# Shift states of a hybrid encoder step written out through TensorE, and half A's first layer norm transposed in the dense PSUM banks

## The chip, the cores and the metric

The kernel is one launch on one core of a Trainium2 chip. The metric is device time in microseconds (us) of that launch. A run's time is that of one execution; the profile is of one more execution. About 0.5% (some 15.5 us here) is the least difference that a measurement of this kernel can tell from none.

## The reference, cut to what matters

A two-layer streaming encoder runs over 1024 new frames of one stream (the prompt, from empty states) and over the next 64 frames of another stream (the sample, from given states). Layer 0 is one input projection that feeds two mixers (RWKV-7 and gated linear attention, GLA), then an output projection; layer 1 is chunk-band attention. Each layer ends with a SwiGLU feed-forward, and each of the four sub-blocks with a layer norm of the residual sum. Everything is float32.

```python
def rwkv7_time_mix(pa, shift0, wkv0, mu, ...):
    prev = jnp.concatenate([shift0[:, None, :], pa[:, :-1]], axis=1)
    xs = pa + (prev - pa) * mu
    ...
    return y, wkv.astype(wkv0.dtype), pa[:, -1]      # pa[:, -1]: the shift state, 1792 numbers

# run_trunk, per layer
x = layer_norm(DEEPNORM_ALPHA * x + mix, P['ln1_w'][layer], P['ln1_b'][layer])
x = layer_norm(DEEPNORM_ALPHA * x + swiglu(x, ...), P['ln2_w'][layer], P['ln2_b'][layer])
```

Two of the twelve outputs are shift states: the last projected row of mixer A, 1792 numbers, once for the prompt and once for the sample.

## The kernel before

The 1088 tokens are split in two halves. Half A holds the first 384 prompt frames and the 64 sample frames (448 columns), half B the other 640 prompt frames. TensorE (PE) works in fp32 split in a high and a low part, so every dense product is three matmuls: high by high, high by low, low by high (lines 124 to 126 with weights stationary, 135, 136 and 138 with tokens stationary). The weights' split is one ACT cast (L101) and one subtraction on DVE (L106) or GpSimd (POOL, L108).

The order in the first part of the program: input projection of half A (`inproj_rwkv`, `inproj_gla`), the mixers of half A beside it, input projection of half B, and then, from about 540 us, three kinds of work woven together: the mixers of half B (the generators `r` for RWKV, 20 units of two 64-token chunks for four head pairs, and `g` for GLA, 20 units), the output projection of half A (`proj(0, ...)`, matrix `w_om`), its layer norm (`layer_norm(0, acc0, "ln1", 0)`), and from there the feed-forward of half A (`ffn(0, 0, ...)`). The program gives the work in that order of text; the framework's scheduler then lays out a fixed order for each engine by its own estimate of times. Each engine runs its list in order and waits on semaphores, so an instruction that waits holds everything behind it on its engine. Nearly all transfers are issued by SyncE (SP), in order too. Each transfer takes one of eight completion semaphores in turn, and the issue of a transfer waits until the earlier one with the same semaphore has landed.

**Shift states.** `shift_evac` copies the last column of each of the 14 projected tiles, one number per partition, into `shS` (sample, L284) and `shP` (prompt, L290), each 128 partitions by 14. Lines 1377 and 1378 write them to the outputs, which are 14 rows of 128: with partitions along the row, each transfer consists of 1792 pieces of 4 bytes.

**PSUM.** The eight banks are given by tags. `gp` has three banks in rotation (`bank()`, tile name `gps`): every dense product takes one, and it is free again when DVE or ACT has read it. `sp_ps` has five banks for the mixers (`sbank(name)`): one for tag a (`pa`, `pb`, `pt`), one for b (`pz`), two for c (`ps`, `py`), one for d (GLA's `gpa`, `gps`, `gpy`). The GLA products are also named `gps`; they are lines 738 to 740.

**The layer norm** of a token tile (line 875 on): statistics on DVE (L884, L886), 1/std on POOL (L888, L889), scaling in two halves (DVE L892, then ACT L894 and POOL L895 for the first half, DVE L897 for the second), then for each half four transposes on PE (L902) into a bank that `self.tpsum()` gives, and the split of the transposed half into high and low (ACT L113, DVE L114), which is the feed-forward's input. In this part `tpsum` is `sbank("tps")`, which falls to tag d, the one bank of GLA.

**The projection** runs over its matrix in two groups of 4 row blocks; per group and token tile it has two products of 512 columns (12 matmuls each), each added to the residual by DVE (L825 in the first group, L827 in the second, L829 for the sample tile's second part). After the second product of a token tile in the second group comes `after(i)`, the layer norm of that tile. Half A has four token tiles, so the norm has eight transposed halves.

```python
for i, t0, m in toks:
    for nh in range(2):
        part(ws[nh], nh, i, t0, m)     # bank(), 12 matmuls, DVE add
    after(i)                           # layer norm of the tile: two tpsum() banks
```

Of the kernel before, what the change touches and what calls it, by code (L numbers as in the profile page):

```python
# [10 lines left out]
F32 = mybir.dt.float32  # L11
# [10 lines left out]
NM = max(NA, NB)  # L22
# [61 lines left out]
class Kern:  # L84
# [134 lines left out]
    def mixer_consts(self, pool, tmp):  # L219
        nc, V = self.nc, self.V  # L220

        def ld(n, src, shape, dt=F32):
            t = pool.tile(shape, dt, name=n, tag=n)
            (nc.sync if n == "vec" else nc.sync).dma_start(t, src)
            setattr(self, n, t)
            return t

        vec = ld("vec", self.a["vec"], [128, NVEC])
        for n, (o, w) in VO.items():
            setattr(self, n, vec[:, o : o + w])  # L230

        def mk(n, src, s, b):
            t = pool.tile([128, src.shape[1]], F32, name=n, tag=n)
            V.tensor_scalar(t, src, s, b, op0=ALU.mult, op1=ALU.add)
            setattr(self, n, t)

        nc.sync.dma_start(self.ident, self.a["c_ident"])
        mk("omu", self.mu, -1.0, 1.0)
        mk("w0h", self.w0, 0.5, 0.0)
        mk("a0h", self.a0, 0.5, 0.0)  # L240
        mk("kah", self.ka, 0.5, 0.0)
        mk("kah1", self.ka, -0.5, 1.0)
        mk("gnwh", self.gnw, 0.5, 0.0)
        self.shA = pool.tile([128, 14], F32, name="shA", tag="shA")
        self.shS = pool.tile([128, 14], F32, name="shS", tag="shS")
        self.shP = pool.tile([128, 14], F32, name="shP", tag="shP")
        for n, sh in (("bdk", [128, 128]), ("mab", [128, 128]), ("mup", [128, 128]), ("mk2", [128, 128]), ("m65", [128, 130]),
                      ("m64", [128, 128]), ("s8", [128, 32]), ("eye16", [16, 256])):
            ld(n, self.a["c_" + n], sh)
        self.u8 = pool.tile([128, 192], U8, name="u8", tag="u8")  # L250
        raw = tmp.tile([128, NM], F32, tag="sq", name="u8raw", bufs=3)[:, :192]
        nc.sync.dma_start(raw, self.a["c_u8"])
        V.tensor_copy(self.u8, raw)
        z = tmp.tile([128, NM], F32, tag="sq", name="zero", bufs=3)[:, :256]
        self.G.memset(z, 0.0)
        for i in range(self.NSL):
            nc.sync.dma_start(self.mats(self.t_d[i], 2), z.rearrange("p (c f) -> p c f", c=2))
            nc.sync.dma_start(self.s_d[i].rearrange("(p f) -> p f", p=128), z[:, : 2 * SST // 128])
        for n in ("w2z", "a2z", "g2"):
            ld(n, self.a[n], [128, 512])  # L260
        self.bd = self.bdk
        self.bd3 = self.bd.rearrange("p (b s) -> p b s", b=2)
# [1077 lines left out]
    def run(self):  # L1340
        nc, tc, a = self.nc, self.tc, self.a
# [17 lines left out]
        one = es_one.enter_context(tc.tile_pool(name="one", bufs=1))  # L1359
# [14 lines left out]
        self.load_xt(1)  # L1374
        self.inproj_gla(1, one)
        self.inproj_rwkv(1, one)
        nc.sync.dma_start(a["s_shift"].rearrange("c p -> p c"), self.shS)
        nc.sync.dma_start(a["p_shift"].rearrange("c p -> p c"), self.shP)
        es_one.close()
        self.load_xt(0, self.yg_d, (4, 5, 6, 7, 0, 1, 2, 3), pool=yp)  # L1380
        es_yr.close()
# [14 lines left out]
        for _ in range(self.PRE):  # L1396
            next(r)
            next(g)
        self.proj(0, acc0, "w_om", self.layer_norm(0, acc0, "ln1", 0), pa)
        for _ in r:  # L1400
            next(g, None)
        for _ in g:
# [212 lines left out]
```

## Time and profile before

| what | value |
|---|---|
| runs, us | 3109.51, 3102.37, 3113.97 (median 3109.51) |
| profiled execution, us | 3102.95 |
| its span, first to last instruction, us | 3101.2 |
| mean granted TensorE clock, share of full speed | 0.977 |
| PE busy, us (share of span) | 3007.5 (97%) |
| DVE busy | 2016.0 (65%) |
| POOL, ACT busy | 1366.7 (44%), 1270.8 (41%) |

The profiled execution is 6.6 us (0.2%) below the median of the runs and 0.6 us above the fastest of them. A busy PE is not a PE at its peak: the granted clock has two levels, 2.4 GHz (1.0 in the rows) and 1.2 GHz (0.5), and a matmul at the lower one takes nearly twice as long. In the rows below PEld is TensorE's weight load and SPq a transfer's issue on SP's queue; `out<-in` are the program's tiles.

### The profile page before, as it was taken

What the parts mean: (1) busy time and instruction counts of PE and PEld (TensorE: products, weight loads), DVE (VectorE), ACT (ScalarE), POOL (GpSimd) and SP (SyncE); (2) the same over time, 40 slices, a digit from 0 to 9 for tenths busy, and PEclk for the clock granted to TensorE, in tenths of its full rate; (3) what the DMA queues carried; (4) which work ended last, traced back from release to release, by engine and by line L of the source; (5) the groups of instructions that cost most, each with busy time, mean ns of one, the idle gap of its engine ahead of it and who ended that gap; (6) DMA issues with size and microseconds to landing.
All of it is one profiled execution on the core that took longest, in us unless ns stands there. A gap on an engine that the chain in (4) does not pass through costs nothing.

```text
span 3101.2 us, 50069 instructions
## 1 busy us (share of the span) xinstructions
PE 3007.5 (97%) x17468; PEld 2676.5 (86%) x17468; DVE 2016.0 (65%) x4941; ACT 1270.8 (41%) x2761; POOL 1366.7 (44%) x1489
## 2 busy tenths in 40 slices
PE   8999999899999999999999999999999999899998
PEld 7888888688888888798999898898899988899987
DVE  5677875879898764455554466245566668866667
ACT  4454554344454334243443132355444434333322
POOL 2354534444454334343342233244445546654444
PEclk9999999889999999999999999999899999999999
DMA  6553334533533228343342222866454443322212
GB/s 195 148 161 115 109 110 124 146 104 106 151 105 106 91 97 294 118 153 120 113 134 98 82 95 101 247 200 175 121 153 135 117 175 122 122 86 80 98 68 75
DMA packets 298492, 399.29 MB, mean 129 GB/s; under 512 B 125504, under 2 KB 218552, under 8 KB 298240
## 3 DMA queue, kind: packets, MB, share of 16 engines
q1 hardware_dynamic: 297088, 393.48, 41.2%
q8 instruction: 138, 2.26, 0.3%
q10 hardware_dynamic: 1152, 2.62, 0.2%
q14 instruction: 114, 0.93, 0.1%
HBM read 323.63 MB, written 75.51 MB: 129 GB/s over the span
## 4 chain that ended last, share of the span: by engine, by line
PE 77%; DVE 8%; DMA 7%; POOL 2%; issue 2%; ACT 2%; SPq 1%; POOLq 0%; ACTq 0%; DVEq 0%
PE gps L124 11%; PE gps L126 11%; PE gps L125 11%; PE gps L135 7%; PE gps L136 7%; PE gps L138 7%; PE gps L1065 3%; PE gps L1066 3%; PE gps L1067 3%; PE op L1328 2%; PE tp L1302 2%; DVE t L549 1%; DVE x L551 1%; PE sps L1286 1%; PE sps L1287 1%
## 5 line engine op out<-in xcount | busy, mean ns | idle before, releaser
L108 POOL TENSOR_TENSOR wl<-wr,wh 128x512 fp32r<-128x512 f32 (+2 forms) x297 | 521.7, 1760 | 669.3 <-ACT wh L101 612.0
L124 PE MATMUL gps<-xh,wh 128*128 128x320 f32 (+1 forms) x2188 | 747.7, 342 | 12.5 <-ACT xh L215 6.0
L125 PE MATMUL gps<-xl,wh 128*128 128x320 f32 (+1 forms) x2188 | 746.5, 341 | 0.6 <-DVE xl L216 0.6
L126 PE MATMUL gps<-xh,wl 128*128 128x320 f32 (+1 forms) x2188 | 745.9, 341 | 0.3 <-DVE wl L106 0.2
L101 ACT CAST wh<-wr 128x1024 fp32r<-128x1024 f32 x360 | 375.6, 1048 | 465.9 <-PE gps L125 135.6
L106 DVE TENSOR_TENSOR wl<-wr,wh 128x512 fp32r<-128x512 f32 (+2 forms) x297 | 293.8, 990 | 242.2 <-ACT wh L101 239.8
L124 PEld LDWEIGHTS gps<-xh,wh 128*128 128x128 f32 x2188 | 415.6, 190 | 34.4 <-ACT xh L215 6.0
L126 PEld LDWEIGHTS gps<-xh,wl 128*128 128x128 f32 x2188 | 415.6, 190 | 18.6 <-issue 0.8
L125 PEld LDWEIGHTS gps<-xl,wh 128*128 128x128 f32 x2188 | 415.5, 190 | 18.3 <-DVE xl L216 1.0
L1297 POOL TENSOR_SCALAR s<-s,mx 128x640 f32<-128x640 f32 (+5 forms) x144 | 205.3, 1426 | 258.7 <-DVE mx L1296 236.3
L138 PE MATMUL gps<-wh,xl 128*128 128x512 f32 x661 | 258.9, 397 | 5.4 <-DVE xl L216 4.8
L135 PE MATMUL gps<-wh,xh 128*128 128x512 f32 x661 | 259.9, 399 | 3.9 <-DVE acc L829 1.9
L136 PE MATMUL gps<-wl,xh 128*128 128x512 f32 x661 | 261.5, 397 | 0.0
L135 PE MATMUL gps<-wh,hh 128*128 128x512 f32 x572 | 224.8, 396 | 1.6 <-ACT wh L101 1.3
L136 PE MATMUL gps<-wl,hh 128*128 128x512 f32 x572 | 225.5, 396 | 0.0
L827 DVE TENSOR_TENSOR acc<-acc,gps 128x512 f32<-128x512 f32 x216 | 143.6, 680 | 89.6 <-PE gps L138 82.3
L138 PE MATMUL gps<-wh,hl 128*128 128x512 f32 x484 | 189.6, 397 | 1.6 <-DVE hl L943 1.6
L549 DVE TENSOR_TENSOR t<-lt,x 16x48 f32<-16x48 f32 (+9 forms) x540 | 149.3, 276 | 36.0 <-DMA lt<-l_d 25.5
L1295 ACT ACTIVATE s<-s,mx 128x640 f32<-128x640 f32 (+5 forms) x144 | 96.4, 669 | 149.6 <-DVE mx L1294 145.2
L138 PEld LDWEIGHTS gps<-wh,xl 128*128 128x128 f32 x661 | 124.9, 189 | 33.8 <-DVE xl L216 5.4
L135 PEld LDWEIGHTS gps<-wh,xh 128*128 128x128 f32 x661 | 125.0, 190 | 32.8 <-issue 2.5
L136 PEld LDWEIGHTS gps<-wl,xh 128*128 128x128 f32 x661 | 125.2, 189 | 28.0 <-DVE wl L106 1.1
(406 smaller groups left out, 6312.0 us busy)
## 6 DMA issues: line engine op xcount, KB each, us to landing
wr<-in_w_fi SPq DMA_DIRECT2D x176, 512.0 KB
wr<-in_w_fo SPq DMA_DIRECT2D x88, 512.0 KB
wr<-in_w_in SPq DMA_DIRECT2D x44, 512.0 KB
wr<-in_w_qk SPq DMA_DIRECT2D x32, 512.0 KB
wr<-in_w_o SPq DMA_DIRECT2D x24, 512.0 KB
qs<-qd SPq DMA_DIRECT2D x32, 320.0 KB
wr<-in_w_om SPq DMA_DIRECT2D x16, 512.0 KB
wr<-in_w_v SPq DMA_DIRECT2D x16, 512.0 KB
```

What stands on the lines that cost most here:

```text
L101: self.A.copy(hi, raw)
L106: self.V.tensor_tensor(lo[:, :h], raw[:, :h], hi[:, :h].bitcast(F32), op=ALU.subtract)
L108: self.G.tensor_tensor(lo[:, h:], raw[:, h:], hi[:, h:].bitcast(F32), op=ALU.subtract)
L124: self.T.matmul(ps, hi[:, kt, :], xh, start=(kt == 0), stop=False)
L125: self.T.matmul(ps, hi[:, kt, :], xl, start=False, stop=False)
L126: self.T.matmul(ps, lo[:, kt, :], xh, start=False, stop=(kt == nk - 1))
L135: self.T.matmul(ps, xh, wh, start=(i == 0), stop=False)
L136: self.T.matmul(ps, xh, wl, start=False, stop=(lo is None and i == n - 1))
L138: self.T.matmul(ps, cols(lo(kt)), wh, start=False, stop=(i == n - 1))
L549: V.tensor_tensor(tv, lt[:, j, w:16].unsqueeze(2).to_broadcast([m, r, w]), x[:, 0, j, 0:w].unsqueeze(1).to_broadcast([m, r, w]), op=ALU.mult)
L827: self.V.tensor_tensor(a, a, ps[:m], op=ALU.add)
L1297: G.tensor_scalar(s[:m, :nk], s[:m, :nk], mx[:m, 3:4], None, op0=ALU.mult)
```

## The change

Both shift states share one tile `shO`, 128 by 28. After half B's input projection PE transposes it into a dense bank, ACT copies the 28 by 128 result to SBUF, and two transfers write 14 rows of 512 bytes each. The sample's state, whose transfer was issued at 92 us before, now leaves with the prompt's. The second edit sets `tpsum` to `bank` while the projection of half A with its layer norm is laid out, so that the eight transposed halves take their banks from the three of `gp`, and sets it back for what follows.

```diff
-        self.shS = pool.tile([128, 14], F32, name="shS", tag="shS")
-        self.shP = pool.tile([128, 14], F32, name="shP", tag="shP")
+        self.shO = pool.tile([128, 28], F32, name="shO", tag="shO")
+        self.shS, self.shP = self.shO[:, 0:14], self.shO[:, 14:28]
...
         self.inproj_rwkv(1, one)
-        nc.sync.dma_start(a["s_shift"].rearrange("c p -> p c"), self.shS)
-        nc.sync.dma_start(a["p_shift"].rearrange("c p -> p c"), self.shP)
+        ps = self.bank()[:28, :128]
+        self.T.transpose(ps, self.shO, self.ident)
+        t = one.tile([128, NM], F32, tag="sq", name="sho", bufs=3)[:28, :128]
+        self.A.copy(t, ps)
+        nc.sync.dma_start(a["s_shift"], t[0:14])
+        nc.sync.dma_start(a["p_shift"], t[14:28])
...
         for _ in range(self.PRE):
             next(r)
             next(g)
+        self.tpsum = self.bank
         self.proj(0, acc0, "w_om", self.layer_norm(0, acc0, "ln1", 0), pa)
+        self.tpsum = lambda: self.sbank("tps")
         for _ in r:
             next(g, None)
```

In the changed kernel the new transpose is line 1378, its ACT copy line 1380 and the two transfers lines 1381 and 1382. Up to here the orders of all engines are the same but for the sample's transfer; from here to the end of half A's feed-forward they differ, and again where attention of half B is woven with the last feed-forward of half A.

The first place is SP's list at the end of half B's input projection (`rkv_d` is the projected row in DRAM, `w_om` the projection's weights, `cv` a piece of the value cache). Before:

```order
L303 DMA rkv_d<-xs 128x640
L1378 DMA out_dram<-shP 128x14x1
L98 DMA wr<-in_w_om 128x1024
L427 DMA rkv<-rkv_d 128x3x128
L654 DMA yg_d<-y 128x128
L1128 DMA vd<-cvh 128x512
L1125 DMA cv<-in_ck_v 128x4x64
```

The same place now:

```order
L303 DMA rkv_d<-xs 128x640
L98 DMA wr<-in_w_om 128x1024
L1381 DMA out_dram<-sho 14x128
L1382 DMA out_dram<-sho 14x128
L427 DMA rkv<-rkv_d 128x3x128
L654 DMA yg_d<-y 128x128
L1128 DMA vd<-cvh 128x512
L1125 DMA cv<-in_ck_v 128x4x64
```

The weights move ahead, and two row transfers stand where the one of 4-byte pieces stood.

The second place is PE's list in the layer norm of half A. Before, a stretch after the last projection product, with two of the eight transposed halves (L902, tile `tps`) among mixer work:

```order
L611 MATMUL ps<-sv,ro 64x64 x2
L484 MATMUL pb<-ar,bbk 128x128 x4
L615 MATMUL ps<-rr,btt 64x64 x2
L902 MATMUL tps<-ident,acc 128x128 x4
L618 MATMUL ps<-uv,tok 64x64 x2
L621 MATMUL ps<-sv,ro 64x64
L622 MATMUL ps<-uv,arb 64x64
```

Now, the second token tile's two halves, and behind them the projection of the third tile:

```order
L510 MATMUL pt<-th,bdk 128x128
L511 MATMUL pt<-ident,rkv 128x128
L902 MATMUL gps<-ident,acc 128x128 x4
L615 MATMUL ps<-rr,btt 64x64
L611 MATMUL ps<-sv,ro 64x64 x2
L738 MATMUL gps<-gv,gba 128x128
L739 MATMUL gps<-gS,gbqk 128x128
L740 MATMUL gps<-gv,gkt 128x128
L615 MATMUL ps<-rr,btt 64x64
L902 MATMUL gps<-ident,acc 128x128 x4
L135 MATMUL gps<-wh,xh_69 128x512
L136 MATMUL gps<-wl,xh_69 128x512
```

Before, the last six of the eight halves stood behind all of the projection; now each token tile's two halves stand ahead of the next tile's products in the second group. Counted in the lists from the end of half B's input projection to the last transposed half, DVE's list has one more RWKV unit and four more GLA units (L549 and L551, the small steps of RWKV's triangular inverse, rise from 37 and 38 to 56 each; L729, one per GLA unit, from 2 to 6; L487, one per RWKV unit, from 3 to 4), and so has PE's.

The third place is PE's list at the start of the output projection. Before:

```order
L649 MATMUL py<-ident,on 128x128
L135 MATMUL gps<-wh,xh_69 128x512
L136 MATMUL gps<-wl,xh_69 128x512
L138 MATMUL gps<-wh,xl_70 128x512
L135 MATMUL gps<-wh,xh_69 128x512
```

And now:

```order
L649 MATMUL py<-ident,on 128x128
L611 MATMUL ps<-sv,ro 64x64 x2
L1378 MATMUL gps<-ident,shO 28x128
L135 MATMUL gps<-wh,xh_69 128x512
L136 MATMUL gps<-wl,xh_69 128x512
```

The new transpose, which needs the last L290 copy, stands ahead of the projection's first product.

## Rows read from the trace of the kernel before

**Rows 1.** The page's busy times, engine, share of the span and instructions, and the granted clock in 40 slices.

```profile
PE 3007.5 (97%) x17468; PEld 2676.5 (86%) x17468; DVE 2016.0 (65%) x4941; ACT 1270.8 (41%) x2761; POOL 1366.7 (44%) x1489
PEclk9999999889999999999999999999899999999999
```

**Rows 2.** SP's queue in order of time, 91 to 108 us: start, duration of the issue, line, transfer.

```profile
92.18 0.43 SPq L1377 DMA_DIRECT2D out_dram<-shS  x1
...
103.70 0.33 SPq L369 DMA_DIRECT2D qkl_d<-abz  x1
```

**Rows 3.** What SP waited for, 92 to 104 us: us in total, times, longest.

```profile
SPq L369 <- DMA out_dram<-shS: 5.1, 1, 5.1
```

**Rows 4.** The DMA view of 92 to 104 us: packets and bytes of the stretch.

```profile
DMA packets 2026, 0.54 MB, mean 45 GB/s; under 512 B 1824, under 2 KB 1952, under 8 KB 2026
```

**Rows 5.** Stretches in us from the span's start: length, then busy time and instructions of PE, PEld, DVE, ACT, POOL, then the granted clock, DMA share and GB/s.

```profile
92.00:104.00 12.00, 11.84 (x59) 10.04 (x58) 7.98 (x24) 10.14 (x25) 6.05 (x15) 1.00 0.73 45
...
111.00:120.00 9.00, 7.51 (x33) 6.59 (x33) 7.75 (x34) 5.14 (x14) 2.69 (x6) 0.81 0.68 229
532.00:539.80 7.80, 2.97 (x11) 1.98 (x11) 5.35 (x14) 5.06 (x15) 4.18 (x4) 0.88 0.13 28
539.80:548.70 8.90, 8.87 (x41) 6.83 (x39) 6.22 (x27) 0.97 (x3) 2.70 (x5) 0.91 0.97 110
548.70:556.70 8.00, 0.00 (x0) 0.00 (x0) 0.66 (x3) 1.09 (x4) 0.30 (x1) 0.68 0.68 160
556.70:565.20 8.50, 6.73 (x28) 5.96 (x29) 7.22 (x26) 4.20 (x15) 3.87 (x10) 0.50 0.80 245
565.20:607.00 41.80, 41.73 (x223) 34.43 (x221) 39.33 (x98) 15.32 (x40) 20.87 (x26) 1.00 0.51 144
607.00:641.60 34.60, 28.66 (x137) 22.66 (x136) 30.28 (x81) 15.64 (x45) 23.33 (x30) 0.54 0.33 115
641.60:1120.00 478.40, 475.85 (x2926) 408.06 (x2925) 392.90 (x1237) 211.81 (x603) 215.49 (x333) 0.99 0.37 109
```

**Rows 6.** What PE waited for, 104 to 120 us.

```profile
PE pa L437 <- DVE bon L520: 1.5, 1, 1.5
```

**Rows 7.** SP's queue, 538 to 552 us.

```profile
540.44 0.42 SPq L1378 DMA_DIRECT2D out_dram<-shP  x1
...
549.68 0.36 SPq L427 DMA_DIRECT2D rkv<-rkv_d  x1
...
551.14 0.43 SPq L1125 DMA_DIRECT2D cv<-in_ck_v  x1
```

**Rows 8.** The chain of waits that ended last, in order of time, between 520 and 680 us: start, us, what.

```profile
527.78 4.91 DMA l_d<-lab
...
539.88 9.74 DMA rkv_d<-xs
```

**Rows 9.** ACT in order of time, 542 to 557 us, with the idle time before in brackets.

```profile
555.61 0.40 ACT L113 CAST cvh<-cv 128x256 fp32r<-128x256 f32 x1 [11.90 <-DMA cv<-in_ck_v]
...
556.43 0.26 ACT L445 COPY gt<-pa 128x128 f32<-128x128 f32 x1
```

**Rows 10.** What PE waited for, 539 to 642 us.

```profile
PE pb L484 <- ACT gt L445: 8.1, 1, 8.1
...
PE tps L902 <- DVE xl L114: 1.1, 2, 0.6
```

**Rows 11.** The same stretch as a whole (539.8 to 641.6 us), columns as in rows 5.

```profile
539.80:641.60 101.80, 85.98 (x425) 69.88 (x424) 83.71 (x230) 37.22 (x105) 51.07 (x70) 0.77 0.52 141
```

**Rows 12.** DVE's groups of instructions in that stretch: busy us, mean ns, then the idle time before them and what ended it.

```profile
L551 DVE TENSOR_TENSOR x<-x,t 16x60 f32<-16x60 f32 (+7 forms) x38 | 12.2, 320 | 0.4
L549 DVE TENSOR_TENSOR t<-lt,x 16x55 f32<-16x55 f32 (+7 forms) x38 | 12.0, 316 | 0.4
...
L114 DVE TENSOR_TENSOR cvh<-cv,cvh 128x256 fp32r<-128x256 f32 x3 | 1.3, 419 | 9.5 <-ACT cvh L113 9.5
...
L758 DVE SCALAR_TENSOR_TENSOR gy<-gpy,gnwh,gsg 128x128 f32<-128x128 f32 x3 | 1.0, 336 | 0.0
...
L744 DVE SCALAR_TENSOR_TENSOR gS<-gps,geb,gse 128x128 f32<-128x128 f32 x2 | 0.7, 328 | 0.0
...
L729 DVE TENSOR_TENSOR gba<-gpa,mup 128x128 f32<-128x128 f32 x2 | 0.6, 282 | 0.0
```

**Rows 13.** PE's groups at full clock, 700 to 900 us: a dense one, and the first and the last of GLA's six (L738, L739, L740, L725, L756, L727, together 19.4 us, with rows that overlap), columns as in rows 12.

```profile
L136 PE MATMUL gps<-wl,hh 128*128 128x512 f32 x60 | 24.5, 408 | 0.0
...
L738 PE MATMUL gps<-gv,gba 128*128 128x128 f32 x18 | 3.9, 298 | 0.0
...
L727 PE MATMUL gpa<-ident,gbqk 128*128 128x128 f32 x9 | 2.5, 279 | 0.0
```

**Rows 14.** 700 to 900 us, columns as in rows 5: all engines, then PE alone and only its instructions that write a `gps` tile (the dense products and L738 to L740), whose row leaves the other engines out.

```profile
700.00:900.00 200.00, 198.44 (x1270) 170.82 (x1269) 179.06 (x595) 97.27 (x298) 102.34 (x172) 0.99 0.43 124
...
700.00:900.00 200.00, 132.91 (x583) 0.99 0.43 124
```

**Rows 15.** DVE's groups in 700 to 900 us that belong to no mixer: the first and the last of eight (L106, L943, L825, L827, L933, L937, L829, L945, together 45.0 us), columns as in rows 12.

```profile
L106 DVE TENSOR_TENSOR wl<-wr,wh 128x1024 fp32r<-128x1024 f32 x12 | 14.5, 1211 | 0.8 <-ACT wh L101 0.8
...
L945 DVE TENSOR_TENSOR hh<-ht,hh 128x64 fp32r<-128x64 f32 x8 | 2.1, 260 | 0.0
```

## The prediction

> **What bounds the kernel now.** I read the busy times first: PE is busy 97% of the span and its granted clock is near full in every slice but a few [rows 1]. So an edit can gain only where PE stands idle or runs at the lower clock, and it loses where it makes new such places. Next I looked at the places that the change touches: SP's queue, what waits there, and the stretches around them.
>
> The sample's shift state is issued at 92.18 [rows 2]. In 92 to 104 us the queues moved 0.54 MB in 2026 packets, 1824 of them under 512 B [rows 4], at 45 GB/s with the DMA engines 0.73 busy [rows 5]: 1792 of these are the transfer's 4-byte pieces. SP waited 5.1 us for it [rows 3] and issued L369 only at 103.70 [rows 2]. What depends on that transfer comes late, and PE shows a wait of 1.5 us for `bon` [rows 6] and a clock of 0.81 in 111 to 120 [rows 5].
>
> The prompt's is issued at 540.44 [rows 7], right behind `rkv_d`, which now takes 9.74 us where a mixer's transfer shortly before took 4.91 [rows 8]. SP's next issue, L427, comes at 549.68, and `cv` at 551.14 [rows 7]. ACT, in order, stands 11.90 us before the cast of `cv`, and `gt`, queued behind that cast, comes at 556.43 [rows 9]. PE waits 8.1 us for `gt` [rows 10]; it does nothing in 548.7 to 556.7 and comes back at 0.50 of its clock until 565.2 [rows 5]. DVE idles 9.5 us at the same cast [rows 12].
>
> From there to the last transposed half of the norm at 641.6 it is DVE that is full: 39.33 of 41.8 us and 30.28 of 34.6, while PE's clock falls to 0.54 in the second stretch with PE idle 6 us of it [rows 5]. The whole stage is 101.8 us with DVE busy 83.71 [rows 11]: 18.1 idle, 9.5 in the one stall, 8.6 elsewhere. From 641.6 to 1120 PE is nearly full again [rows 5].
>
> **The sample's state leaves the early queue.** L369 is issued some 5 us earlier. The wait of 1.5 us goes, and so does half-clock time: at a mean of 0.81, 38% of 9 us ran at 1.2 GHz, 3.4 us, of which full clock gives half back, 1.7. Gain 3 (0, if another transfer is late in its place, to 3.2).
>
> **The prompt's state in rows.** Two transfers of 7 KB in 512-byte rows take its place. With `rkv_d` taking about 4.9 instead of 9.74, L427 is issued near 544.8 and `cv`, two issues on, near 546.3. It landed 4.5 us after its issue before (555.61 less 551.14), so now near 550.7, and `gt` near 551.6, 4.8 us earlier. DVE's stall of 9.5 shrinks to about 5 (0 to 9.5), and PE's of 8.1 to about 3, or less with the displaced products below.
>
> **The new transpose** heads PE's list before the projection and needs the last shift copy, which comes when half B's projection ends, at 539.8. Until then PE worked 2.97 us in 7.8 [rows 5], on seven products that now queue behind it. That work moves into the stage. It costs up to 3; 0 if it fills PE's remaining stall. I take 2, since PE's first products also feed the first adds on DVE. The ACT copy and the two issues are about as large as the `gt` copy's 0.26 and an issue's 0.42 [rows 7, 9], under a microsecond on engines that wait here anyway: 0.
>
> **The norm in the dense banks.** What the edit can remove directly is PE's wait for a `tps` bank, 1.1 us [rows 10]. What it adds is an order. The three `gp` banks go round in text order: per token tile two products, then two transposed halves. The next tile's second product gets the bank of this tile's first half, and that is free only when DVE has split it. So products and norm alternate, and the scheduler has put more mixer work between: one RWKV unit, a quarter of the inverse of another, and four GLA units.
>
> DVE's price for these: in 700 to 900 us it is busy 179.06 [rows 14], of which 45.0 is not mixers [rows 15]. A GLA unit is six instructions of about 0.315 (the mean of three of them in rows 12), 1.9 us; nine make 17.1. The rest, 117, is eight RWKV units of 14.6. So 14.6, and 4 x 1.9 = 7.6, and for the part inverse about 6.6 instructions (37 more in the lists, against some 30 in a unit) of 0.318 [rows 12], 2.1: 24 together (21, if 0.87 of it, which is the stage's busy 83.7 over the sum 95.9 of its rows).
>
> PE's credit, work done in the stage that before came later: in 700 to 900 us PE is busy 198.44, 132.91 of it on `gps` tiles, so the mixers take 65.5 beside L738 to L740 [rows 14]. GLA's six groups sum to 19.4 us, nine units of at most 2.2 [rows 13]. PE's rows overlap there (they sum to 1.6 times the busy time), so I take 1.3. Eight RWKV units then have about 60, 7.5 each. One RWKV unit and four GLA units: 7.5 + 5.3 = 13 (10 to 16).
>
> The new stage is then DVE's 83.7 + 24, its other idle time of 8.6, the remaining stall of 5, and waits for banks. The three handovers from one tile to the next are new; nothing in the trace shows them. Their nearest rows are the 1.1 us of `tps` [rows 10] below and, above, one product of 12 matmuls that runs exposed, 12 x 0.408 = 4.9 [rows 13] each time, some 13 for three. I take 2, since mixer work stands between. Together 123 (111, if the idle time closes too, to 139). Net: 123 - 101.8 - 13 = **+8** (-7 to +27).
>
> The Trainium skill speaks against this edit: "Perfetto Trace Analysis", section "Matmuls", wants independent groups to rotate through different banks, so that their evacuation overlaps the next group's matmuls. Here eight more evacuations go through the three `gp` banks, where the norm had another. By the rule the waits come to their upper end and the time to about 3122; by the 1.1 us of rows 10, which are of the order before, to 3110.
>
> **Later.** With mixer work done earlier, 641.6 to 1120 can close its holes: PE is idle 2.6 us there, and 0.01 of 478 us missing from the clock is 4.8 [rows 5]. Up to -7; I take -2. The other order late in the program has a PE that is full: 0.
>
> **Sum.** -3 + 2 + 8 - 2 = **+5** on the profiled execution's 3102.95, 3108. That execution is 6.6 below the median of the runs and near the fastest; I carry half of that and forecast **3111 us**. Its own range is 3099 to 3123.
>
> **Rivals.**
>
> *The banks bind (slower).* Each of the three handovers makes PE wait for ACT's cast and DVE's split while DVE in turn waits for products, and short bursts keep PE at 1.2 GHz, as in 607 to 641.6 where the clock was 0.54 [rows 5]. It decides when a handover costs over 4 us: W is 138 instead of 123, later holes stay, and the sum is -3 + 2 + 23 = +22, about 3128 with the carry. For it: DVE is full in this stage. Against it: five units of mixer work fill the gaps, and POOL and ACT are half idle [rows 11].
>
> *The stage packs (faster).* DVE's idle time falls away since more units are at hand: W is 111, net -4, later relief -7, the sum -3 + 1 - 4 - 7 = -13, about 3093. For it: 83.7 of 101.8 leaves room. Against it: the norm is one chain through DVE, POOL, ACT and PE, and the second stretch left 4.3 of 34.6 us idle with mixers at hand [rows 5].
>
> *The pieces are not the cause (no gain in the queue).* `cv`, `rkv_d` and the weights `wr` meet in 539.8 to 548.7, where the DMA share is 0.97 [rows 5]. If their bytes hold the queue, the stall stays at 9.5 and the early 3 us too: 3111 + 3 + 4.5, about 3118. Against it: 110 GB/s there, 245 in 556.7 to 565.2 [rows 5]; the engines were busy with few bytes. A rule of the Trainium skill ("DMA: Bandwidth & Descriptors", section "Bandwidth", measured) is on its side: some 10.5 ns a packet. By it an estimate for 1792 packets on 16 engines is 1.2 us, which would make each transfer cheap; the traffic of rows 4 and 5 near 92 us, almost all of it these packets for some 10 us, does not agree.
>
> **Chances.** Forecast 0.65, banks bind 0.15, stage packs 0.13, pieces not the cause 0.07. A measurement of this kernel can tell about 0.5% from no change, 15.5 us, so no change is 3094 to 3125. Most of the slower rival lies above it, and the upper tail of the forecast's bounds adds little; slower 0.15. About all of the packing rival is at its edge, with bounds that go to -17; faster 0.13. No change 0.72. The range of 3092 to 3129 takes in both rivals' centres and leaves out the ends of the bounds.
>
> **What would show it.** In the changed profile SP has no wait of 5 us near 98, and PE none for `bon` near 111. L427 is issued near 545 and PE's wait for `gt` is under 4 us. The first products come behind L1378, with about 7 us of PE idle before 539.8. The last split of the norm is near 663 instead of 641.6, with DVE over 85% busy in between and one RWKV and four GLA units more in it. PE's waits for banks on DVE's `xl` sum to 1 to 5 us; over 12 speaks for the slower rival. I am wrong if the last split lies before 650 or after 680, or if L427 is still issued after 548.

## The result, and the profile after

The changed kernel takes 3116.11 us (median of 20 runs, 3110.08 to 3121.59) beside 3105.19 of the kernel before (20 runs, 3100.56 to 3115.52): a ratio of 1.0031, 95% interval 1.0022 to 1.0039. By the ratio that is 9.6 us slower (6.8 to 12.1). The profiled execution has a span of 3109.0 and lies at the lower end of its runs, so a part of the loss is not in its trace.

**The queue.** SP's list in 92 to 100 us of the changed kernel (start, duration, line, transfer), and its waits there:

```profile
...
95.93 1.09 SPq L434 DMA_DIRECT2D rsb<-rs_d  x2
98.59 0.34 SPq L369 DMA_DIRECT2D qkl_d<-abz  x1
```

```profile
...
SPq L369 <- POOL abz L368: 1.5, 1, 1.5
...
```

L369 leaves at 98.59 where it left at 103.70 [rows 2], and waits for its own data alone [rows 3]. PE's clock has a low stretch in this trace too, 0.74 in 92 to 104 us; in the kernel before it lay in 111 to 120 [rows 5]. The last section shows that its place is not the edit's doing. (Columns as in [rows 5].)

```profile
92.00:104.00 12.00, 12.00 (x44) 9.53 (x43) 5.26 (x18) 8.54 (x18) 3.73 (x10) 0.74 0.26 80
104.00:120.00 16.00, 16.00 (x85) 14.12 (x84) 13.01 (x41) 10.48 (x22) 8.94 (x12) 1.00 0.54 178
```

**The stall.** SP and ACT of the changed kernel at the end of half B's projection:

```profile
539.76 0.38 SPq L1382 DMA_DIRECT2D out_dram<-sho  x1
542.64 0.40 SPq L427 DMA_DIRECT2D rkv<-rkv_d  x1
...
544.62 0.43 SPq L1125 DMA_DIRECT2D cv<-in_ck_v  x1
```

```profile
548.23 0.41 ACT L113 CAST cvh<-cv 128x256 fp32r<-128x256 f32 x1 [5.64 <-DMA cv<-in_ck_v]
...
549.89 0.26 ACT L445 COPY gt<-pa 128x128 f32<-128x128 f32 x1
```

L427 leaves 7.0 us earlier [rows 7], 1.7 of it because half B's projection ends at 538.1 instead of 539.8. ACT stands 5.64 us instead of 11.90 before the cast, and `gt` comes 6.5 us earlier [rows 9]. What PE and DVE wait for in 538 to 660 us:

```profile
PE gps L135 <- issue: 4.0, 1, 4.0
PE py L649 <- ACT on L642: 3.9, 2, 2.2
PE gps L1378 <- DVE shO L290: 3.8, 1, 3.8
PE gpa L725 <- DVE gy L758: 2.7, 1, 2.7
PE gpy L756 <- ACT gon L754: 2.6, 1, 2.6
...
PE pb L484 <- ACT gt L445: 1.3, 2, 0.9
...
```

```profile
DVE cvh L114 <- ACT cvh L113: 3.7, 2, 2.4
```

PE's 8.1 us for `gt` [rows 10] are 1.3, DVE's 9.5 [rows 12] are 3.7. The new transpose waits 3.8. The longest row, 4.0, stands ahead of the first product on `xpk` (L135); "issue" means that the profile names nothing that ended it. None of PE's thirteen rows there is a wait for a bank (on DVE's `xl`); most are waits inside the mixers.

**The stage**, from the last shift copy to the last split of the norm, and from there to half A's second norm; columns as in [rows 5], the kernel before first:

```profile
539.80:641.20 101.40, 85.58 (x424) 69.52 (x423) 83.31 (x228) 37.22 (x105) 50.70 (x70) 0.77 0.53 141
```

```profile
538.10:657.50 119.40, 98.31 (x534) 80.13 (x534) 103.32 (x311) 49.11 (x154) 62.15 (x100) 0.83 0.46 131
657.50:1158.40 500.90, 499.18 (x2990) 428.34 (x2989) 392.26 (x1187) 211.65 (x569) 210.72 (x314) 0.99 0.37 108
```

DVE is busy 103.3 us instead of 83.3 and the stage is 119.4 instead of 101.4 (each to the start of the last split). It has 110 PE instructions more than before, and what follows is 13 us shorter.

**Where the time went.** Five places that every kernel here has divide the execution: the last shift copy (end of half B's projection), the start of the norm's last split, the first transposed half of half A's second norm that goes to a `ps` bank (some 3 us behind its very first), the last transposed half of half B's, which is the last in a `gps` bank in the profile, and the end. The lengths, us:

| kernel | to the shift copy | to the last split | to half A's second norm | to half B's norm | to the end |
|---|---|---|---|---|---|
| before | 539.8 | 101.4 | 514.1 | 1487.0 | 458.9 |
| changed | 538.1 | 119.4 | 500.9 | 1487.3 | 463.3 |
| difference | -1.7 | +18.0 | -13.2 | +0.3 | +4.4 |

So in this trace the stage that the prediction was about leaves +4.8 net, and another 4.4 comes from the last stretch, which the prediction put at 0. The order there hangs on one line of the program: `bank()` counts its calls, and once the last part has its second set of five banks, `self.bcount % 8 > 2` deals the products out to the two sets. The transpose takes one bank and the norm eight, so the count is nine higher, one modulo eight.

### The profile page after: what moved, and what is told of

Its sections match the earlier page's. It is cut to its first block, busy times and chain, and to the rows that moved or that the text cites. A ratio compares the mean times of both kernels' runs of the same rounds, so it can differ in the third digit from the quotient of the medians.

```text
span 3109.0 us, 50085 instructions
## 1 busy us (share of the span) xinstructions
PE 3012.4 (97%) x17469; PEld 2677.1 (86%) x17469; DVE 2013.4 (65%) x4941; ACT 1273.4 (41%) x2762; POOL 1354.7 (44%) x1489
## 4 chain that ended last, share of the span: by engine, by line
PE 80%; DVE 7%; DMA 6%; POOL 3%; issue 2%; ACT 2%; SPq 1%; POOLq 0%; ACTq 0%; DVEq 0%
PE gps L124 11%; PE gps L125 11%; PE gps L126 11%; PE gps L135 8%; PE gps L136 8%; PE gps L138 7%; PE gps L1067 2%; PE gps L1065 2%; PE gps L1066 2%; PE op L1328 2%; PE tp L1302 2%; DMA wr<-in_w_in 1%; PE ps L622 1%; PE sps L1286 1%; PE sps L1287 1%
## 5 line engine op out<-in xcount | busy, mean ns | idle before, releaser
L106 DVE TENSOR_TENSOR wl<-wr,wh 128x512 fp32r<-128x512 f32 (+2 forms) x297 | 293.7, 989 | 240.1 <-ACT wh L101 235.8
L135 PE MATMUL gps<-wh,xh 128*128 128x512 f32 x661 | 258.3, 399 | 3.8 <-DVE acc L829 1.9
L135 PE MATMUL gps<-wh,hh 128*128 128x512 f32 x572 | 227.0, 398 | 2.3 <-DVE ht L937 2.0
L827 DVE TENSOR_TENSOR acc<-acc,gps 128x512 f32<-128x512 f32 x216 | 143.4, 679 | 84.5 <-PE gps L138 78.5
L549 DVE TENSOR_TENSOR t<-lt,x 16x48 f32<-16x48 f32 (+9 forms) x540 | 149.3, 276 | 39.0 <-DMA lt<-l_d 28.5
L135 PEld LDWEIGHTS gps<-wh,xh 128*128 128x128 f32 x661 | 124.8, 189 | 32.2 <-issue 2.3
```

What stands on the lines that cost most here:

```text
L106: self.V.tensor_tensor(lo[:, :h], raw[:, :h], hi[:, :h].bitcast(F32), op=ALU.subtract)
L135: self.T.matmul(ps, xh, wh, start=(i == 0), stop=False)
L549: V.tensor_tensor(tv, lt[:, j, w:16].unsqueeze(2).to_broadcast([m, r, w]), x[:, 0, j, 0:w].unsqueeze(1).to_broadcast([m, r, w]), op=ALU.mult)
L827: self.V.tensor_tensor(a, a, ps[:m], op=ALU.add)
```

## The experiments

Theories at the start: (1) the loss sits in the last part's order, which the counter shifts; (2) it sits in the norm's banks. In the edits below, "counter put back" is the one line of the first diff. Expectations count the last stretch to the last down product, some 13 us short of the end that the table above uses. Ratios are to the kernel before, run on the same chip in the same job (medians 3103.38, 3106.12 and 3104.55).

### Two edits and the counter, apart

```diff
 # before_count: the kernel before
         self.inproj_rwkv(1, one)
+        self.bcount += 1
 # shift_count, after_count: counter put back
         ps = self.bank()[:28, :128]
+        self.bcount -= 1
 # banks_only: the second edit alone; shift_only, shift_count: the first alone
-        self.tpsum = self.bank
         self.proj(0, acc0, "w_om", self.layer_norm(0, acc0, "ln1", 0), pa)
-        self.tpsum = lambda: self.sbank("tps")
```

**before_count.** 

> Kernel before with one line added: the counter of dense banks goes up by one after half B's input projection, as the new transpose does, with no other work. That counter (bcount % 8 > 2) deals the products of the last part out to two sets of banks, so only the order near the end changes. Theory 1 (the loss sits in that later order): 4 to 9 us slower than before, with the time up to about 2500 us as before. Theory 2 (the loss sits in the layer norm that takes its banks from the dense rotation): within 2 us of before.

Measured: 1.0018 (1.0009 to 1.0027), 5.5 us. PE's waits in the last stretch, first of before_count, then of the changed kernel with the counter put back (after_count), which has the order of the kernel before:

```profile
PE gps L1065 <- DVE c L1082: 4.6, 2, 2.5
PE gps L1065 <- ACT c L1076: 3.4, 1, 3.4
PE gps L1067 <- DVE wl L1038: 2.7, 3, 1.5
PE gps L1066 <- POOL xl L114: 2.0, 1, 2.0
...
```

```profile
PE gps L1065 <- ACT wh L1037: 5.4, 1, 5.4
PE gps L1065 <- ACT c L1076: 2.3, 1, 2.3
...
```

The order that the shifted counter gives makes PE wait for other operands of the last feed-forward (`c`, `wl`), and at more places. No work was added: one count of one counter costs 4.4 us of span in that stretch (463.3 beside 458.9).

**shift_count.** 

> Shift states transposed and stored in rows, layer norm in its old bank, and the bank counter put back by one after the transpose, so that the last part has the order of before. Both theories: 1 to 6 us faster than before (the wait at 92 us and the stall at 549 us are gone); theory 1 says that the same kernel without the counter put back would be some 7 us slower than this one.

Measured: 0.9977 (0.9968 to 0.9987), 7.1 us faster, a little above the expected range. The stage, from shift copy to last split, is 95.3 us instead of 101.4 (the stretch behind it is the second row):

```profile
536.30:631.60 95.30, 82.50 (x418) 67.14 (x419) 84.81 (x226) 37.74 (x105) 46.91 (x69) 0.80 0.51 151
631.60:1146.30 514.70, 510.86 (x3104) 439.35 (x3103) 417.97 (x1272) 221.39 (x619) 227.49 (x344) 0.99 0.37 107
```

**banks_only.** 

> Only the layer norm of half A in the dense banks; shift states in 4-byte pieces as before. It takes eight more banks, so the counter's remainder by 8 and the last part's order are those of before. Theory 1: 2 to 6 us slower than before, by the longer stage alone. Theory 2: 9 to 14 us slower.

Measured: 1.0065 (1.0053 to 1.0078), 20 us slower: above what either theory gave.

```profile
539.50:658.30 118.80, 93.36 (x488) 76.25 (x487) 94.86 (x281) 44.84 (x139) 59.56 (x93) 0.82 0.51 127
658.30:1171.00 512.70, 508.17 (x3032) 433.74 (x3032) 402.45 (x1216) 212.21 (x583) 210.44 (x320) 0.99 0.36 106
```

PE is idle 25.4 us in the stage beside 15.8 in the same stage before (101.40 us, busy 85.58). The 64 PE instructions done early give back 1.4 us at most: the stretch behind takes 512.7 instead of 514.1, and before_count, the list of the kernel before in that stretch, has 512.7 as well.

**after_count.** 

> The changed kernel whole, with the bank counter put back by one after the transpose, so that the last part has the order of before. Theory 1: 0 to 4 us slower than before, 5 to 9 faster than the changed kernel. Theory 2: as the changed kernel, 8 to 12 us slower than before.

Measured: 1.0027 (1.0018 to 1.0037), 8.4 us slower. So theory 1 falls as the whole cause: with the last stretch mended (459.0), most of the loss stays. The ratios of this pair (1.0027 and 1.0031) do not tell the counter's 4 us by themselves; the last stretch does. Beside shift_count, the banks cost 0.5%, 15.5 us:

```profile
539.00:659.50 120.50, 100.44 (x534) 82.08 (x534) 103.86 (x312) 49.08 (x154) 61.76 (x100) 0.80 0.46 130
659.50:1164.30 504.80, 502.15 (x2989) 431.30 (x2988) 392.26 (x1187) 212.49 (x569) 210.11 (x314) 0.99 0.37 107
```

The stage is 25.2 us longer than shift_count's, and the stretch behind it 9.9 shorter (504.8 beside 514.7). Up to the last part this is the program of the changed kernel, whose two stretches sum to 620.3 where these sum to 625.3: one program differs by 5 us there between two executions, and the changed kernel's trace shows its cheaper one.

**shift_only.** 

> The shift edit alone, the norm in its old bank, nothing done to the bank counter. With the counter put back it ran at 0.9977 of before. Theory of the counter: 4 to 5.5 us slower than that, 2 to 4 us under before (0.999), last stretch 450 us. Rival: 7 to 8 us under before.

Measured: 0.9983 (0.9975 to 0.9992), 5.3 us under before, between the two expectations. The interval covers shift_count's, so the ratios alone don't tell them apart; the last stretch does, with 462.9 against 459.5.

### What makes the norm's banks cost

Theory A: the order. Theory B: the banks by themselves, since the products have fewer.

```diff
 # after_defer, defer_plain (tsg, the branch of half A's projection)
             for i, t0, m in toks:
                 for nh in range(2):
                     part(ws[nh], nh, i, t0, m)
-                after(i)
+                if not self.defer:
+                    after(i)
+                elif last is not None:
+                    after(last)
+                last = i
+            if self.defer:
+                after(last)
 # after_half (the caller; the counter is put up by four as well)
+        def norm(i):
+            self.tpsum = self.bank if i < 2 else lambda: self.sbank("tps")
+            ln(i)
```

**after_defer.** 

> The changed kernel with the bank counter put back, and the norm of each token tile in half A's projection laid out one tile later: after the next tile's two products instead of ahead of them. The norm still takes its eight halves from the dense banks. In DVE's list the last split then stands 76 instructions earlier than without that. Theory A (the loss of about 15 us beside the shift edit alone comes from the order: products and norm alternate through three banks, and the next product waits behind the norm): most of it goes, the time is 8 to 2 us under before, and the last split of the norm comes some 15 us earlier. Theory B (the dense banks cost by themselves, since dense products have fewer of them): it stays, 5 to 9 us over before.

Measured: 0.9967 (0.9951 to 0.9983), 10 us faster, a little more than theory A gave. The last split starts 94.5 us after the shift copy instead of 120.5, with the same eight halves in the same three banks:

```profile
536.60:631.10 94.50, 81.24 (x442) 66.66 (x443) 85.22 (x237) 40.58 (x118) 52.28 (x77) 0.88 0.53 155
631.10:1139.30 508.20, 507.81 (x3081) 436.28 (x3081) 414.65 (x1262) 220.48 (x606) 224.11 (x336) 1.00 0.37 108
```

The same banks in another order cost nothing here: theory A holds for this pair, and B falls. In PE's list the next tile's products now stand ahead of the norm's transposes, and 92 fewer PE instructions of other work lie in the stage. With the norm in its old bank (a list that was laid out and not run), the same deferral leaves PE's list row for row as shift_count's: with a bank of its own the norm goes behind the products in either order of the text. Only where both draw on one rotation does the text's order bind the list. With the transpose moved (defer_late, below) the deferral does not help, so the result is not a general one.

**after_half.** 

> The changed kernel with the counter put back, and the dense banks for the norm of the first two of half A's four token tiles only; the other two take the old bank. Theory A: the cost goes with the handovers, of which one or two of three are left, so 4 us under to 4 over before. Theory B: four halves of eight, half of the cost, likewise about 0; this run tells only whether the cost goes with the number.

Measured: 1.0029 (1.0017 to 1.0041), 9 us slower: a miss for both theories, which gave about 0. Half of the halves cost as much as all of them.

```profile
536.50:646.40 109.90, 92.04 (x456) 74.37 (x457) 94.61 (x273) 40.64 (x115) 50.89 (x75) 0.78 0.45 131
646.40:1163.30 516.90, 511.05 (x3067) 436.49 (x3066) 403.61 (x1226) 219.21 (x608) 221.88 (x339) 0.99 0.37 107
```

The stage is 14.6 us longer than shift_count's with only 38 PE instructions more, and nothing comes back behind it. So the cost does not go with the number of halves, nor with the mixer work in the stage; why two tiles give the whole of it is not shown.

**defer_plain.** 

> The changed kernel with the norm laid out one token tile later, and nothing done to the bank counter: the last part has the order of the changed kernel. The same kernel with the counter put back ran at 0.9967 of before. If the later order costs 4 to 5.5 us whatever comes ahead of it (theory: it is a matter of that counter alone), this one runs 6 us under before (0.998), and its last stretch, from half B's last norm transposes to the end, takes some 450 us instead of 446. Rival: the order's cost came from what was ahead of it; then the same time as with the counter put back.

Measured: 0.9986 (0.9977 to 0.9996), 4.3 us under before, last stretch 463.1: nearer to the counter's theory than to the rival.

### The parts of the shift edit, and a better kernel

```diff
 # p_rows_count: the sample's state as before, the prompt's in rows
+        nc.sync.dma_start(a["s_shift"].rearrange("c p -> p c"), self.shS)
         ps = self.bank()[:28, :128]
 ...
-        nc.sync.dma_start(a["s_shift"], t[0:14])
 # shift_late, defer_late, defer_late_4: the six lines behind half A's projection
         self.proj(0, acc0, "w_om", self.layer_norm(0, acc0, "ln1", 0), pa)
+        ps = self.bank()[:28, :128]
+        self.bcount -= 1        # defer_late_4: += 3
+        ...
```

**p_rows_count.** 

> Only the prompt's shift state is transposed and leaves in rows; the sample's leaves early in 4-byte pieces as before; norm in its old bank, bank counter put back. With both in rows the kernel was 7 us faster than before. By the stages some 2.5 us of it lie ahead of the end of half B's projection and 5 to 6 behind it: this run 4 to 6 us faster than before if the two parts add up, and SP's wait of 5 us near 98 is back. If the sample's transfer is worth nothing (rival: its waits are hidden), 7 to 8 us faster.

Measured: 0.9980 (0.9968 to 0.9992), 6.2 us, between the two. The wait is back:

```profile
SPq L369 <- DMA out_dram<-shO: 6.0, 1, 6.0
...
```

The end of half B's projection comes at 541.3. Over the four kernels with the early transfer of 4-byte pieces (before, before_count, banks_only, this one) it lies at 540.7 on average, over the ten with rows at 538.0. The ten scatter from 534.5 to 541.0, so the sample's share, 2.7 us in the means, is known to about 2 us either way and no closer (an estimate from that scatter).

**shift_late.** 

> Both shift states in rows, norm in its old bank, counter put back, but the transpose and its two transfers stand behind half A's projection and norm instead of ahead of them, so that no product waits for the last shift copy. By the prediction's step (the transpose at the head of PE's list costs up to 3 us): 1 to 3 us faster than with the transpose at the head, 8 to 11 faster than before. Rival: those products only fill a stall that comes anyway; no difference, 7 to 8 faster.

Measured: 0.9967 (0.9955 to 0.9979), 3 us under shift_count with intervals that overlap. From the shift copy to half A's second norm its trace has 612.7 us, shift_count's 610.0: the trace does not show the gain. Undecided.

**defer_late.** 

> Norm in the dense banks one token tile later, counter put back, and the transpose of the shift states behind half A's projection and norm. If the two gains add up (10 us from the first, 1 to 3 from the transpose): 11 to 14 us under before, the fastest of all. If the first products fill a stall anyway: 9 to 11 under.

Measured: 0.9997 (0.9987 to 1.0006). A miss: the gains don't add. Its two stretches sum to 619.5, those of after_defer and defer_plain, one program there, to 602.7 and 610.7. Moving one transpose reorders the stage anew: 427 PE instructions instead of 442 lie in it, at 0.82 of the clock instead of 0.88:

```profile
534.50:634.40 99.90, 82.41 (x427) 66.76 (x426) 87.56 (x238) 37.96 (x113) 50.91 (x74) 0.82 0.48 141
634.40:1154.00 519.60, 515.96 (x3093) 440.50 (x3093) 414.90 (x1261) 222.83 (x609) 222.42 (x341) 0.99 0.37 107
```

Beside shift_late, which has the same late transpose and the norm in its old bank (0.9967), the dense banks cost 0.3% here, 9 us, although the norm is deferred. The stage is not where it lies (99.9 beside 98.7); the stretch behind it takes 519.6 beside 514.0, in one trace each. So the deferral does not always make the sharing free, and why this list is the worse one stays open.

**defer_late_4.** 

> As the one before, but the bank counter moved on by four in all (put up by three after the transpose) instead of put back: another deal of the last part's products to the two sets of banks. Theory of the counter: only the last stretch differs from that kernel's; it is a third draw of that order, 446 us if the order of before was no special one, up to 450 or more if it was.

Measured: 0.9998 (0.9989 to 1.0007), last stretch 458.8. Of the three remainders tried, two give a last stretch of some 459 us; the one that the change fell on is the bad one.

The fastest kernels are after_defer and shift_late, both at 0.9967: 10 us under the kernel before and 0.6%, some 20 us, under the changed one (1.0031).

## Why the prediction was right, and where not

The forecast of 3111 with 3092 to 3129 holds 3116, "no change within 0.5%" was the likeliest case and came, and the sign of the sum (+5) is the measured one (+9.6). That the sum came so near is in part luck: the shift edit gave 4.1 us more than forecast behind half B's projection, and the late order took 3.8 that were not forecast. By its steps, with the mean of kernels that run the same program in a stretch:

| step | predicted | measured |
|---|---|---|
| sample's state leaves the early queue | -3 | -2.7 (538.0 against 540.7), known to some 2 us |
| prompt's state in rows, the stall, the transpose | -4.5 + 2 | -6.6 (609.4 of the shift kernels against 616.0, shift copy to half A's second norm) |
| norm in the dense banks, with what comes back | +12.5 - 2 | +13.4 (622.8 against 609.4) |
| late order | 0 | +3.8 (463.2 in four kernels, 459.4 in the others) |
| sum | +5 | +8 |

- **The sample's state: the size fits, the reason given for it does not.** The 3 us were PE's wait of 1.5 for `bon` and the clock of 0.81 in 111 to 120 us [rows 5, 6]. In before_count, whose lists are those of the kernel before up to the last part, 4-byte pieces included, PE does not wait for `bon` there and the clock is 1.00 in 111 to 120 (rows in the last section). The prediction took for a cost of the transfer what one execution showed.
- **The queue and the stall of the prompt's state: right.** L427 at 542.6 (forecast 545), PE's wait for `gt` 1.3 us (under 4), DVE's stall 3.7 (5). The rival that the pieces are not the cause falls: with rows the stall shrinks, and where only the prompt's pieces go (p_rows_count) the stage is 95.5 us like shift_count's 95.3. By the Trainium skill's packet price ("DMA: Bandwidth & Descriptors", section "Bandwidth") such a transfer would have been an estimated 1.2 us, divided over 16 engines as in the prediction; the section does not say that its price is one engine's, and undivided the estimate is 18.8 us. SP's wait of 6.0 us for it in p_rows_count does not agree with the 1.2: issued at 90.90 us, it held L369 until 103.30.
- **The transpose at the head of PE's list**: its wait shows (3.8 us), its price doesn't. It was put at 2; in the sum of the stage the shift edit gains 6.6, more than the forecast with the transpose at 0. A second idle stretch goes with it that the prediction did not have: the 4.0 us ahead of the first product on `xpk` stand in all eight kernels with the transpose at the head (3.4 to 4.5), and 0 to 0.7 in the six others. Whether that is time lost is not shown; the stage of shift_late, which is without it, is not shorter.
- **The stage: right in its parts.** DVE is busy 103.3 (forecast 107.7), other idle time 16.1 (15.6), last split 119.4 us after the shift copy (123), one RWKV and four GLA units more. What came back was 9.9 to 13.2 us of the 13 forecast and 2 of later relief.
- **Waits for banks: wrong in kind.** I looked for waits of PE on DVE's `xl`, 1 to 5 us, and priced three handovers. None shows. With the norm in its old bank there is one: 3.6 us in shift_count (1.1 in the kernel before [rows 10]).

```profile
PE tps L902 <- DVE xl L114: 3.6, 1, 3.6
```

So the edit took away the wait that it was meant to take away, and the kernel lost all the same. The rotation acted before the run: it bound the order of the lists and let the scheduler put other work into the gap, and PE is idle 21.1 us of the stage (20.1 in after_count), mostly on operands of the mixers, beside 12.8 in shift_count. That the loss runs through these waits is read from the rows and not tested by itself. The slower rival has the right place and the wrong mechanism. The rule that I set beside it (the Trainium skill, "Perfetto Trace Analysis", section "Matmuls") wants groups in different banks; after_defer, with the same banks and another order, shows that here the order decided, not how many banks there are; by defer_late it does not decide alone.

- **The late order: the term that failed.** "The other order late in the program has a PE that is full: 0." PE is full over most of it, but the list changes where it is not: behind half B's norm. The kernel before has PE idle 9.7 of the 57.7 us there and full in the next 100; with the count shifted (before_count, the second pair) the next 100 lose 4.8 us too:

```profile
2642.30:2700.00 57.70, 48.01 (x269) 0.88 0.39 128
2700.00:2800.00 100.00, 100.00 (x597) 1.00 0.28 98
```

```profile
2644.80:2702.50 57.70, 47.97 (x277) 0.91 0.41 137
2702.50:2802.50 100.00, 95.25 (x556) 0.98 0.25 81
```

Over the four pairs that differ in the counter alone, the ratios give 5.5, 1.2, 1.9 and 5.9 us (before, changed, shift and deferred kernel), the last stretches 3.4 to 4.4. I had seen that the lists differ there and did not ask why; the counter's line would have told.

## What to carry to other kernels

When two streams of work take buffers from one rotation, their order in the text can become an order on the chip even if no wait for a buffer ever shows it: try the consumer laid out one step behind before judging the sharing, and time it again when something near it moves, since here it helped with the transpose at the head and not with the transpose late. A counter that deals out buffers by a remainder is a hidden input of everything behind it, so an edit that takes one buffer more should put it back, or be timed with it apart. And before a small change is judged, split it: here some -7 us, +15 us and +4 us hid under one "no change".

## What was not expected of the hardware

Where PE's granted clock falls near 100 us changes between executions of one list. First before_count, whose lists are there those of the kernel before, then the changed kernel, then shift_count, whose lists are there those of the changed kernel:

```profile
80.00:92.00 12.00, 9.36 (x51) 7.12 (x49) 7.08 (x21) 4.36 (x11) 4.83 (x4) 1.00 0.56 174
92.00:104.00 12.00, 11.77 (x40) 9.20 (x41) 5.27 (x18) 8.55 (x22) 4.71 (x12) 0.72 0.73 44
111.00:120.00 9.00, 9.00 (x50) 7.91 (x49) 8.12 (x38) 5.15 (x14) 1.91 (x8) 1.00 0.66 207
```

```profile
80.00:92.00 12.00, 10.00 (x51) 7.38 (x51) 8.20 (x26) 5.45 (x16) 5.66 (x7) 0.98 0.59 199
```

```profile
80.00:92.00 12.00, 11.84 (x61) 8.89 (x59) 8.14 (x27) 5.83 (x17) 5.42 (x9) 1.00 0.59 195
92.00:104.00 12.00, 12.00 (x64) 11.12 (x64) 7.12 (x25) 10.51 (x19) 4.75 (x10) 1.00 0.37 118
```

The clock is 0.72 in 92 to 104 us with the early transfer in place, after 2.6 us of PE idle in 80 to 92; it is 0.74 without the transfer after 2.0 us of idle, and 1.00 without it after 0.2. So the low stretch came with idle time ahead of it in these traces, and neither its place nor its presence is the edit's doing.

One program also differs by 5 to 8 us between executions from the shift copy to half A's second norm (620.3 and 625.3; 602.7 and 610.7), so single traces tell steps of that size only together with ratios.
